# Spreading the inverse RMS roots of a decoder block: transpose, mask and one matmul of ones in place of eight matmuls

## The chip, the cores and the metric

The kernel runs on one core of a Trainium2 chip. The metric is the device time of one execution in microseconds (us). TensorE (PE) does matmuls and transposes, VectorE (DVE), ScalarE (ACT) and GpSimd (POOL) do elementwise work, and SyncE (SP) starts most DMAs. Each engine works through its own queue in order.

## The reference

One layer with 2048 tokens and 1024 channels, in float32. All four RMS norms have this form, over 1024 or 512 channels:

```python
def rmsnorm(x, g):
    r = lax.rsqrt(jnp.mean(xf * xf, axis=-1, keepdims=True) + EPS)
    return xf * r * g

hn = rmsnorm(h, norm1_g)
proj = einsum('bsd,de->bse', hn, w_in)          # u_pool | q | k | v, 512 channels each
y_pool = pool_mixer(u_pool, pool_w, pool_scale) # causal means over 2, 4, 8, 16 tokens, then 128x128 maps
y_attn = stick_breaking_attention(q, k, v)      # 8 heads of 64
mixed = concat[rmsnorm(y_pool, pool_out_g), rmsnorm(y_attn, attn_out_g)]
h = h + mixed @ w_out
up = rmsnorm(h, norm2_g) @ w_up                 # 4096 channels
h = h + square(relu(up)) @ w_down
return rmsnorm(h, final_g)
```

## The kernel before, in words

Channels lie on the 128 partitions and tokens on the free axis. The 2048 tokens are cut into `NT = 4` chunks of `T = 512`, and each chunk into `TB = 4` blocks of 128. A float32 product is made of three matmuls in the type fp32r: each operand is split by `split` (L145 on ACT, L146 on DVE) into a high and a low part, and high*high, high*low and low*high are summed (L177 to L179). In the text such a matmul of 512 columns, `pd<-h,hl`, is called a dense one.

The program has three stages. The front (to about 500 us) makes the input projection of all chunks, the pool mixer and the near part of the attention, interleaved. Then comes the output projection (to about 690 us), and then the two feed-forward products (names `pY`, `pZ`, `pX`, `pb`).

A norm goes like this. `sum_squares` adds squares over the channel tiles into `ss` (128 x 512). `mean_squares` (L204) makes four matmuls of one column each, which leave the mean square of each token in `pm`, 128 x 4: the tokens of a block are now on the partitions. `inv_root` copies it to SBUF on DVE (`v`, L212) and takes the inverse root in steps of Newton on POOL (L213 to L223). `inv_rms` splits the root into a high and a low part, `yr` (128 x 2 x 4, L240 and L241). `spread` (L230) turns this back into a row of 512 tokens that stands on every partition, `pr` in PSUM, by eight matmuls: for each block and part a column of `yr`, broadcast over 128 columns, is the stationary operand and the identity `identr` the moving one. ACT copies `pr` to `r` in SBUF (L250). `normed` then multiplies the chunk by gain and `r` on DVE (`nt`, L262) and splits it into `h` or `mix`.

In the executed path `inv_rms` runs 14 times: once on DVE alone (the first norm of chunk 0) and 13 times with POOL: norm 1 of chunks 1 to 3, the pool norm and the attention norm of four chunks each, and norm 2 of chunks 0 and 1. The other norms (norm 2 of chunks 2 and 3, the final norm) call `spread` themselves.

The order of instructions on each engine is worked out ahead of time by the framework's list scheduler, from its own estimates; it follows data dependencies, free buffers, priorities (`tc.high_priority` around `inv_rms`) and explicit orders (`tc.issue_after`). Two devices of the kernel set the order around the norms:

- `later` is a queue of small pieces of norm work, of which one to three are written after each projection step.
- `gates` holds pairs of a step count and an instruction: a projection step whose count is past the pair's may only be issued behind that instruction. `inv_rms` gates on its last `pm` matmul (10 granules on) and on its last spread matmul (14 on).

PSUM tiles come from pools with few buffers: `pd` 2, `pz` 2 (attention logits), `pt` 2 (attention transposes `pta`, and `pr`), `px` 1 (`pp` of the pool mixer, transposes of v, `pm`), `po` 1. For chunk 1 (`early`) `pr` comes from `pz` in place of `pt`.

Other names in the rows: `raw` and `hl` are weights before and after their split, `pls` and `pp` input and output of the pool mixer's matmul (L396 to L398), `yb` its copy by ACT (L399), `qkr` and `qk` queries and keys, `kw`, `qa`, `qb`, `sh`, `sg`, `pc`, `at`, `vw` operands and results of the attention, `acc` the residual.

Of the kernel before, what the change touches and what calls it, by code (L numbers as in the profile page):

```python
# [8 lines left out]
F32 = mybir.dt.float32  # L9
F32R = mybir.dt.float32r  # L10
BF16 = mybir.dt.bfloat16
I32 = mybir.dt.int32
AF = mybir.ActivationFunctionType
ALU = mybir.AluOpType

P = 128
S = 2048
D = 1024
T = 512
# [8 lines left out]
TB = T // P  # L28
# [17 lines left out]
def hymba_block(ctx: ExitStack, tc: tile.TileContext, xT, gains, w_in, pool_w, w_out, w_up, w_down, out):  # L46
    nc = tc.nc
# [3 lines left out]
    const = pool("const", 1)  # L51
    vp = pool("vp", 2)
    dram = pool("dram", 1, space=bass.MemoryType.DRAM)
    wp = hpb = hpa = pa = bigp = x0p = ntp = tmp = att = psd = psx = psz = pst = pso = olp = accp = acc2p = acc3p = None

    def open_pools(scope):
        nonlocal hpb, wp, tmp, ntp, psd, psx, psz, pst, pso
        fpool = lambda name, bufs, **kw: scope.enter_context(tc.tile_pool(name=name, bufs=bufs, **kw))
        hpb = fpool("hpb", KD, side="right")
        ntp = fpool("ntp", 3, side="right")  # L60
        tmp = fpool("tmp", 2, side="right")
        wp = fpool("wp", 2, side="right")
        psz = fpool("psz", 2, space=PS)
        pso = fpool("pso", 1, space=PS)
        psd = fpool("psd", 2, space=PS)
        psx = fpool("psx", 1, space=PS)
        pst = fpool("pst", 2, space=PS)
# [19 lines left out]

    front_scope, left_scope, att_scope, out_scope, last_scope, inner = (ctx.enter_context(ExitStack()) for _ in range(6))
    open_pools(front_scope)
    open_big(left_scope)  # L90

# [3 lines left out]
    ident = const.tile([P, P], F32, name="ident")  # L95
    make_identity(nc, ident)
    identr = const.tile([P, P], F32R, name="identr")
    nc.vector.tensor_copy(identr, ident)
    const.tile([P, P // 2], F32, name="gap")
    later_keys = const.tile([P, 2, 2, P], mybir.dt.int8, name="later_keys")  # L100
    nc.gpsimd.memset(later_keys, 0.0)
    for i in range(2):
# [49 lines left out]
    marks, gates = {}, []  # L152
# [46 lines left out]
    def mean_squares(parts, n, where=None, tag="px"):  # L199

        pm = (where or psx).tile([P, T], F32, tag=tag, name="pm")
        for c in range(TB):
            for i, ss in enumerate(parts):
                marks["pm"] = nc.tensor.matmul(pm[:, c:c + 1], ss[:, c * P:(c + 1) * P], inv[n],  # L204
                                               start=(i == 0), stop=(i == len(parts) - 1))
        return pm[:, 0:TB]

    def inv_root(pm, eng):

        v, w = vp.tile([P, 3 * TB], F32, tag="v", name="v"), pm.shape[-1]  # L210
        m, y, t = v[:, 0:w], v[:, TB:TB + w], v[:, 2 * TB:2 * TB + w]
        nc.vector.tensor_scalar(m, pm, 1.0, EPS, op0=ALU.mult, op1=ALU.add)  # L212
        eng.tensor_scalar(y.bitcast(I32), m.bitcast(I32), -0.5, float(0x5F3759DF), op0=ALU.mult, op1=ALU.add)  # L213
        for _ in range(3):
            if eng is nc.vector:
                eng.scalar_tensor_tensor(t, y, -0.5, y, op0=ALU.mult, op1=ALU.mult)
                eng.tensor_tensor(t, t, m, ALU.mult)
                eng.scalar_tensor_tensor(y, t, 1.5, y, op0=ALU.add, op1=ALU.mult)
            else:
                eng.tensor_tensor(t, y, y, ALU.mult)  # L220
                eng.tensor_tensor(t, t, m, ALU.mult)
                eng.tensor_scalar(t, t, -0.5, 1.5, op0=ALU.mult, op1=ALU.add)
                eng.tensor_tensor(y, y, t, ALU.mult)  # L223
        return y

    def spread(pr, yr):

        for b in range(TB):
            for x in range(2):
                mm = nc.tensor.matmul(pr[:, b * P:(b + 1) * P], yr[:, x, b:b + 1].to_broadcast([P, P]), identr,  # L230
                                      start=(b == 0 and x == 0), stop=(b == TB - 1 and x == 1), skip_group_check=True)
        return mm

    def inv_rms(ss, n, r=None, eng=None, early=False):

        eng = eng or nc.gpsimd
        with tc.high_priority():
            y = inv_root(mean_squares([ss], n, psz if early else None, "pz" if early else "px"), eng)
            yr = tmp.tile([P, 2, TB], F32R, tag="yr", name="yr")
            eng.tensor_copy(yr[:, 0], y)  # L240
            eng.tensor_tensor(yr[:, 1], y, yr[:, 0].bitcast(F32), ALU.subtract)  # L241
            where, tag = (psx, "px") if eng is nc.vector else (psz, "pz") if early else (pst, "pt")
            pr = where.tile([P, T], F32, tag=tag, name="pr")
            marks["pr"] = spread(pr, yr)
            if eng is not nc.vector:
                g = state["tick"]
                gates.extend([(g + 10, marks["pm"]), (g + 14, marks["pr"])])
            if r is None:
                r = tmp.tile([P, T], F32, tag="r", name="r", bufs=2)
            nc.scalar.activation(r, pr, AF.Copy)  # L250
            return r

    def rms(chunks):
        return inv_rms(sum_squares(chunks), len(chunks) * P)
# [41 lines left out]
    todo, begun, finished, state = [], {}, set(), {"gran": 0, "tick": 0, "due": 0.0}  # L296
# [37 lines left out]
    def norm1_first():  # L334

        x, h = st[0]["x"], []
        for k in range(KD):
            d = make_h(0)
            a = nc.scalar.activation(d[:, 0], x[:, k], AF.Copy, scale=g1[:, k:k + 1])
            v = nc.vector.scalar_tensor_tensor(d[:, 1], x[:, k], g1[:, k:k + 1], d[:, 0].bitcast(F32),  # L340
                                               op0=ALU.mult, op1=ALU.subtract)
            h.append((d[:, 0], d[:, 1]))
        st[0]["h"] = h
        with tc.issue_after(a.ins), tc.issue_after(v.ins):
            ss = sum_squares([x[:, k] for k in range(KD)])
        st[0]["r"] = inv_rms(ss, D, root_tile(), nc.vector)

    def norm1_rms(j):
        def square(k):
            if k == 0:  # L350
                st[j]["ss"] = sum_tile()
            add_square(st[j]["ss"], st[j]["x"][:, k], k == 0)
        later.extend(lambda k=k: square(k) for k in range(KD))
        later.append(lambda: st[j].update(r=inv_rms(st[j]["ss"], D, root_tile() if j == 2 else None, early=j == 1)))
# [1217 lines left out]
    pa = inner.enter_context(tc.tile_pool(name="pa", bufs=2))  # L1572
    x0p = x0_scope.enter_context(tc.tile_pool(name="x0p", bufs=2, side="right"))
# [69 lines left out]
```

## Time and profile before

| what | value |
|---|---|
| runs of the kernel before | 1900.64, 1901.84, 1903.91 us (median 1901.84) |
| profiled execution | 1901.53 us, of it 1899.8 us span from first to last instruction |
| PE busy | 1873.7 us, 99% |
| DVE, ACT, POOL busy | 1482.2 us (78%), 1025.0 us (54%), 235.1 us (12%) |
| mean granted TensorE clock | 0.996 |
| matmuls of `spread` | 152 (136 on `yr`, 16 on `yrlast`) |

A row of the groups reads: line, engine, operation, out<-in by the program's names, shapes, count | busy us, mean ns of one | idle us of the engine just before, and what ended it. A row of the timeline reads: start in us, length in us, engine, line, operation, count, and in brackets how long the engine had been idle and for whom. The length of a matmul runs to its modelled end, and the next one starts before that; what one costs in a row is the distance of starts.

### The profile page before, as it was taken

How to read it: one execution, taken by the hardware profiler on the slowest of the kernel's cores; microseconds unless marked ns; L12 is line 12 of the kernel's file. 1: busy time of each engine (PE TensorE's matmuls, PEld its weight loads, DVE VectorE, ACT ScalarE, POOL GpSimd, SP SyncE). 2: the span in 40 equal slices, each digit the busy share in tenths (PEclk: the TensorE clock that was granted, in tenths of full speed). 3: DMA queues.
4: the chain of work that ended last, by engine and by line, in shares of the span. 5: the costliest groups of instructions: out<-in, count | busy, mean ns of one | idle time of the engine just before them, and what ended most of it. 6: DMA issues, size and time to landing. Idle time of an engine off the chain costs nothing.

```text
span 1899.8 us, 26686 instructions
## 1 busy us (share of the span) xinstructions
PE 1873.7 (99%) x8883; PEld 1563.1 (82%) x8883; DVE 1482.2 (78%) x2151; ACT 1025.0 (54%) x1616; POOL 235.1 (12%) x463
## 2 busy tenths in 40 slices
PE   9999999999999999999999999999999999999997
PEld 7888888888888888788888888888888888888886
DVE  6887799668866976878799988887666677888774
ACT  6565566555544465455557555554432665656543
POOL 0333234223321020000000000000010010020120
PEclk9999999999999999999999999999999999999998
DMA  7685686898788867787899897889999899999852
GB/s 227 206 282 180 215 278 221 255 322 265 271 300 324 295 233 245 279 316 271 292 358 338 315 302 280 300 280 333 389 309 341 274 321 306 330 302 344 286 209 91
DMA packets 222164, 535.91 MB, mean 282 GB/s; under 512 B 26048, under 2 KB 32192, under 8 KB 218176
## 3 DMA queue, kind: packets, MB, share of 16 engines
q1 hardware_dynamic: 217264, 525.46, 79.4%
q0 software_dynamic: 4608, 8.39, 2.4%
q8 instruction: 72, 1.18, 0.3%
q14 instruction: 76, 0.62, 0.1%
q10 hardware_dynamic: 144, 0.26, 0.0%
HBM read 349.46 MB, written 184.55 MB: 281 GB/s over the span
## 4 chain that ended last, share of the span: by engine, by line
PE 52%; DMA 3%; DVE 2%; issue 1%; ACT 1%; POOL 0%; SPq 0%; DVEq 0%; ACTq 0%
PE pb L1274 16%; PE pY L1101 13%; PE pb L1451 12%; PE pZ L1101 7%; PE pX L1101 3%; DMA hn<-hs 1%; PE pb L1391 1%; DMA su<-hs 0%; DMA td<-t 0%; DMA wr<-in_w_down_dram 0%; DMA b<-in_w_down_dram 0%; DMA ar<-sd 0%; DMA t<-in_w_down_dram 0%; DVE hw L146 0%; DVE a L1060 0%
## 5 line engine op out<-in xcount | busy, mean ns | idle before, releaser
L1101 PE MATMUL pY<-sa,hw 128*128 128x512 f32 x1536 | 366.4, 389 | 2.6 <-ACT u L1024 2.6
L1101 PEld LDWEIGHTS pY<-sa,hw 128*128 128x128 f32 x1536 | 287.9, 188 | 64.0 <-ACT u L1024 4.3
L1274 PE MATMUL pb<-ad,wd 128*128 128x512 f32 x1344 | 304.8, 389 | 0.0
L177 PE MATMUL pd<-h,hl 128*128 128x512 f32 x752 | 298.4, 397 | 1.8 <-ACT vf L437 0.7
L179 PE MATMUL pd<-h,hl 128*128 128x512 f32 x752 | 296.5, 394 | 0.0
L178 PE MATMUL pd<-h,hl 128*128 128x512 f32 x752 | 296.3, 394 | 0.0
L1274 PEld LDWEIGHTS pb<-ad,wd 128*128 128x128 f32 x1344 | 252.3, 188 | 52.4
L1451 PE MATMUL pb<-ad,wd 128*128 128x512 f32 x1104 | 253.8, 390 | 0.6 <-ACT ad L145 0.6
L1451 PEld LDWEIGHTS pb<-ad,wd 128*128 128x128 f32 x1104 | 206.5, 188 | 44.3 <-ACT ad L145 1.0
L146 DVE TENSOR_TENSOR ad<-ar,ad 128x1024 fp32r<-128x1024 f32 x160 | 194.2, 1221 | 41.3 <-ACT ad L145 40.9
L145 ACT ACTIVATE ad<-ar 128x1024 fp32r<-128x1024 f32 x160 | 168.2, 1053 | 91.0 <-PE pb L1451 32.0
L1101 PE MATMUL pZ<-sa,hw 128*128 128x512 f32 x768 | 187.0, 390 | 1.8 <-DVE a L1044 1.8
L1101 PEld LDWEIGHTS pZ<-sa,hw 128*128 128x128 f32 x768 | 143.8, 188 | 33.1 <-DVE a L1044 3.4
L177 PEld LDWEIGHTS pd<-h,hl 128*128 128x128 f32 x752 | 142.1, 189 | 29.8 <-ACT h L145 1.1
L179 PEld LDWEIGHTS pd<-h,hl 128*128 128x128 f32 x752 | 141.8, 189 | 28.5
L178 PEld LDWEIGHTS pd<-h,hl 128*128 128x128 f32 x752 | 142.0, 189 | 26.5
L145 ACT ACTIVATE hl<-raw 128x512 fp32r<-128x512 f32 x168 | 104.0, 630 | 105.6 <-PE pd L179 66.7
L146 DVE TENSOR_TENSOR hl<-raw,hl 128x512 fp32r<-128x512 f32 x168 | 114.3, 686 | 46.1 <-ACT hl L145 41.4
L1018 ACT ACTIVATE a<-a 128x512 f32<-128x512 f32 x96 | 60.1, 629 | 93.1 <-DVE a L1060 40.0
L146 DVE TENSOR_TENSOR hw<-rt,hw 128x512 fp32r<-128x512 f32 x128 | 86.6, 686 | 24.7 <-ACT hw L145 24.6
L145 ACT ACTIVATE wd<-wq 128x1024 fp32r<-128x1024 f32 x56 | 59.4, 1060 | 79.6 <-PE pb L1274 69.2
L146 DVE TENSOR_TENSOR wd<-wq,wd 128x1024 fp32r<-128x1024 f32 x56 | 68.5, 1224 | 35.7 <-ACT wd L145 35.6
(218 smaller groups left out, 2749.3 us busy)
## 6 DMA issues: line engine op xcount, KB each, us to landing
ar<-sd SPq DMA_DIRECT2D x96, 512.0 KB, 5.6
ar<-sdi SPq DMA_DIRECT2D x64, 512.0 KB, 5.6
rb<-in_w_up_dram SPq DMA_DIRECT2D x30, 1024.0 KB, 6.3
sd<-a SPq DMA_DIRECT2D x104, 256.0 KB, 5.1
raw<-in_w_in_dram SPq DMA_DIRECT2D x50, 512.0 KB, 4.4
sdi<-hr SPq DMA_DIRECT2D x96, 256.0 KB, 5.5
wr<-in_w_down_dram SPq DMA_DIRECT2D x48, 512.0 KB, 5.4
sd<-s SPq DMA_DIRECT2D x88, 256.0 KB, 5.0
```

The costliest lines, as they stand in the source:

```text
L145: nc.scalar.activation(hi, src, AF.Copy)
L146: return nc.vector.tensor_tensor(lo, src, hi.bitcast(F32), ALU.subtract)
L177: nc.tensor.matmul(ps, hl[:, 0, c], hi, start=(k == 0), stop=False)
L178: nc.tensor.matmul(ps, hl[:, 0, c], lo, start=False, stop=False)
L179: mm = nc.tensor.matmul(ps, hl[:, 1, c], hi, start=False, stop=(k == n - 1))
L1018: nc.scalar.activation(t, src, AF.Relu)
L1101: nc.tensor.matmul(t, w[:, wx, c], a[:, ax, c % 2], start=first and c == 0 and x == 0, stop=last and c == G - 1 and x == 2, skip_group_che ...
L1274: nc.tensor.matmul(b, t[:, wx, 2 * (kk % 2) + c, i * P:(i + 1) * P], a[:, ax, c], start=p in ("P1", "P5", "P2") and kk == 0 and c == 0 and ...
L1391: nc.tensor.matmul(b[:, cols], block(t, wx, c, n), a[:, ax, c, cols], start=False, stop=(i == 1 and c == 1 and x == 2), skip_group_check=True)
L1451: nc.tensor.matmul(ps[q, n], block(t, wx, c, n), left_[q][:, ax, c], start=(n_ in ("P1", "P3") and kk == 0 and c == 0 and x == 0), stop=(n ...
```

## The change

The 13 calls of `inv_rms` with POOL no longer call `spread` but a new function, `spread_rows`. It transposes `yr`, read as 128 x 8, to 8 rows of 128 tokens (`pr[0:8, 0:128]`, mark `pt8`). ACT copies these rows four times into `roots`, 8 x 512, once for each block of tokens, each time scaled per row by a column of `sel`, which is one for the two rows (high and low) of that block and zero for the others. One matmul with ones, 8 rows and 512 columns, sums the eight rows onto all partitions, into the same tile `pr`. The copy from `pr` to `r` stays. The gate on the last spread matmul moves from 14 to 16, and the transpose gets a gate at 14. The DVE variant, `root_last` and the final norm keep `spread`. Two small constants, `sel` and `oner`, are made by DVE at the start; `gap` shrinks by as much, so that other constants keep their places. `roots` has a pool of its own of 2 KB per partition.

```diff
+        zp = fpool("zp", 1, side="right")
...
-    const.tile([P, P // 2], F32, name="gap")
+    const.tile([P, P // 2 - 8], F32, name="gap")
+    sel = const.tile([P, TB], F32, name="sel")
+    nc.vector.tensor_tensor(sel, ident[:, 0:TB], ident[:, TB:2 * TB], ALU.add)
+    oner = const.tile([P, TB], F32R, name="oner")
+    nc.vector.tensor_scalar(oner, sel, 0.0, 1.0, op0=ALU.mult, op1=ALU.add)
...
+    def spread_rows(pr, yr, r, mark):
+
+        rows, z = 2 * TB, zp.tile([P, T], F32R, tag="roots", name="roots")[0:2 * TB]
+        mm = nc.tensor.transpose(pr[0:rows, 0:P], yr.bitcast(F32).rearrange("p x b -> p (x b)"), ident)
+        marks[mark] = mm
+        for b in range(TB):
+            nc.scalar.activation(z[:, b * P:(b + 1) * P], pr[0:rows, 0:P], AF.Copy, scale=sel[0:rows, b:b + 1])
+        mm = nc.tensor.matmul(pr, oner[0:rows, 0:1].to_broadcast([rows, P]), z, start=True, stop=True)
+        nc.scalar.activation(r, pr, AF.Copy)
+        return mm
...
             pr = where.tile([P, T], F32, tag=tag, name="pr")
-            marks["pr"] = spread(pr, yr)
-            if eng is not nc.vector:
-                g = state["tick"]
-                gates.extend([(g + 10, marks["pm"]), (g + 14, marks["pr"])])
             if r is None:
                 r = tmp.tile([P, T], F32, tag="r", name="r", bufs=2)
-            nc.scalar.activation(r, pr, AF.Copy)
+            if eng is nc.vector:
+                marks["pr"] = spread(pr, yr)
+                nc.scalar.activation(r, pr, AF.Copy)
+            else:
+                marks["pr"] = spread_rows(pr, yr, r, "pt8")
+                g = state["tick"]
+                gates.extend([(g + 10, marks["pm"]), (g + 14, marks["pt8"]), (g + 16, marks["pr"])])
             return r
```

The scheduler works out a new order from this. In the rows below, lines of the changed program are 5 higher than before in the products (L182 to L184 for L177 to L179) and 18 higher from the pool mixer on (L414 to L416 for L396 to L398); L242 is the transpose, L245 the masking, L246 the matmul of ones, L247 the copy to `r`.

On PE, around the first of the 13 (norm 1 of chunk 1), there stands before, with the spread (L230) in the middle:

```order
L178 MATMUL pd<-h,hl 128x512
L179 MATMUL pd<-h,hl 128x512
L230 MATMUL pr<-identr,yr 128x128
L177 MATMUL pd<-h,hl 128x512
L230 MATMUL pr<-identr,yr 128x128 x7
L396 MATMUL pp<-pls,pw 128x512
L397 MATMUL pp<-pls,pw 128x512
L398 MATMUL pp<-pls,pw 128x512
L178 MATMUL pd<-h,hl 128x512
L179 MATMUL pd<-h,hl 128x512
```

At the same place now, with 16 dense matmuls and one `pp` group between the transpose (not shown) and the matmul of ones:

```order
L184 MATMUL pd<-h,hl 128x512
L246 MATMUL pr<-roots,oner 128x512
L414 MATMUL pp<-pls,pw 128x512
L415 MATMUL pp<-pls,pw 128x512
L416 MATMUL pp<-pls,pw 128x512
L414 MATMUL pp<-pls,pw 128x512
L415 MATMUL pp<-pls,pw 128x512
L416 MATMUL pp<-pls,pw 128x512
L182 MATMUL pd<-h,hl 128x512 x2
L183 MATMUL pd<-h,hl 128x512
```

Two groups of `pp`, which share one buffer, now follow each other, and the first of the two L182 is the first matmul that reads the `h` made with this `r`; before, one `pp` group, 17 dense matmuls and another `pp` group stood between the spread and it.

On ACT, at the same place, before:

```order
L145 ACTIVATE pls<-pl 128x512
L145 ACTIVATE hl<-raw 128x512
L250 ACTIVATE r<-pr 128x512
L399 ACTIVATE yb<-pp,gains 128x512
L145 ACTIVATE h<-nt 128x512 x3
L399 ACTIVATE yb<-pp,gains 128x512
```

And now:

```order
L150 ACTIVATE hl<-raw 128x512
L245 ACTIVATE roots<-pr,sel 8x128 x4
L417 ACTIVATE yb<-pp,gains 128x512
L150 ACTIVATE pls<-pl 128x512
L247 ACTIVATE r<-pr 128x512
L150 ACTIVATE qk<-qkr 128x512
L417 ACTIVATE yb<-pp,gains 128x512
L150 ACTIVATE h<-nt 128x512 x2
L417 ACTIVATE yb<-pp,gains 128x512
```

The four masks stand where the copy to `r` stood; that copy now stands behind a `yb` and a `pls`, and a `qk` and a `yb` stand between it and the first `h`.

On POOL, at the end of the root chain of the eighth of the 13 (the attention norm of chunk 1), before:

```order
L223 TENSOR_TENSOR v<-v 128x4
L647 AFFINE_SELECT sg<-sg 128x2x128
L220 TENSOR_TENSOR v<-v 128x4
L659 COPY left_140<-pc 128x2
L221 TENSOR_TENSOR v<-v 128x4
L222 TENSOR_SCALAR v<-v 128x4
L223 TENSOR_TENSOR v<-v 128x4
L240 CAST yr<-v 128x4
L241 TENSOR_TENSOR yr<-v,yr 128x4
```

And now:

```order
L228 TENSOR_TENSOR v<-v 128x4
L225 TENSOR_TENSOR v<-v 128x4
L226 TENSOR_TENSOR v<-v 128x4
L227 TENSOR_SCALAR v<-v 128x4
L228 TENSOR_TENSOR v<-v 128x4
L256 CAST yr<-v 128x4
L257 TENSOR_TENSOR yr<-v,yr 128x4
```

A mask and a copy of the attention, L647 and L659, which stood inside this chain now stand elsewhere. The feed-forward stage has the same order on PE as before, apart from where the two `spread` of `yrlast` stand at its start.

4 lines of the change are left out of this document (2 added, 2 removed).

## The prediction

> **What bounds the kernel now.** I read the page's first part, then the waits of PE, then PE's timeline around the spreads.
>
> ```profile
> span 1899.8 us, 26686 instructions
> PE 1873.7 (99%) x8883; PEld 1563.1 (82%) x8883; DVE 1482.2 (78%) x2151; ACT 1025.0 (54%) x1616; POOL 235.1 (12%) x463
> ...
> PE pY L1101 <- ACT u L1024: 2.6, 4, 1.0
> PE pr L230 <- POOL yr L240: 1.8, 1, 1.8
> PE pZ L1101 <- DVE a L1044: 1.8, 3, 1.0
> ```
>
> PE is busy for 99% of the span and its longest waits (us in total, times, longest) are a few us over the whole program. So what PE no longer issues is saved in full, as long as no new wait takes its place; work of the other engines is free while PE has something to do. One of these few waits is a spread that waits 1.8 us for POOL, and it has a sequel:
>
> ```profile
> 442.67 0.95 PE L204 MATMUL pm<-inv,ss 128*128 128x1 f32 x8
> ...
> 450.93 0.45 PE L179 MATMUL pd<-h,hl 128*128 128x512 f32 x1
> 453.20 2.03 PE L230 MATMUL pr<-identr,yr 128*128 128x128 f32 x8 [1.82 <-POOL yr L240]
> 455.03 1.07 PE L663 MATMUL pta<-ident,sg 128*128 128x128 f32 x4
> 455.76 0.78 PE L177 MATMUL pd<-h,hl 128*128 128x512 f32 x1
> 456.33 0.63 PE L178 MATMUL pd<-h,hl 128*128 128x512 f32 x1
> 456.76 0.63 PE L179 MATMUL pd<-h,hl 128*128 128x512 f32 x1
> ...
> 450.00:452.00 2.00, 1.38 (x12) 1.07 (x10) 1.52 (x3) 1.22 (x2) 1.83 (x7) 1.00 0.97 300
> 452.00:454.00 2.00, 0.80 (x4) 0.77 (x4) 1.09 (x2) 0.00 (x0) 1.77 (x5) 0.82 0.93 342
> 454.00:456.00 2.00, 2.00 (x11) 2.00 (x11) 1.90 (x4) 0.60 (x1) 0.00 (x0) 0.50 0.77 249
> 456.00:460.00 4.00, 4.00 (x11) 3.13 (x11) 3.26 (x5) 1.24 (x2) 0.00 (x0) 0.50 0.83 253
> 460.00:464.00 4.00, 4.00 (x23) 3.38 (x23) 1.35 (x2) 2.50 (x5) 0.34 (x1) 0.99 0.48 134
> ```
>
> The third number from the end of a row of stretches is the granted clock. It is 1.00 up to 452, then falls to 0.50 and is back shortly after 460: 0.72 us of the second stretch, all 6 of the next two and 0.08 of the last, 6.8 us at half speed with PE full of work (11 matmuls in 4 us against 23). That costs 3.4 us. It begins right behind the wait of 1.82 us, and it is the only such stretch that I found in the front and the output projection.
>
> **What is removed: the eight matmuls.** There are 13 places.
>
> ```profile
> 619.61 0.39 PE L179 MATMUL pd<-h,hl 128*128 128x512 f32 x1
> 619.83 1.00 PE L230 MATMUL pr<-identr,yr 128*128 128x128 f32 x8
> 620.67 0.45 PE L177 MATMUL pd<-h,hl 128*128 128x512 f32 x1
> 620.96 0.39 PE L178 MATMUL pd<-h,hl 128*128 128x512 f32 x1
> 621.19 0.39 PE L179 MATMUL pd<-h,hl 128*128 128x512 f32 x1
> ```
>
> Starts of dense matmuls are 0.23 us apart (620.96 to 621.19). From 619.83 to 620.96 PE passes eight spread matmuls and one dense: 1.13 less 0.23 is 0.90 us a place.
>
> **What is added on PE: a transpose and a matmul of 512 columns.** The nearest rows are the transposes of the attention, which run in groups of four:
>
> ```profile
> 184.85 0.63 PE L663 MATMUL pta<-ident,sg 128*128 128x128 f32 x4
> 185.23 0.48 PE L396 MATMUL pp<-pls,pw 128*128 128x512 f32 x1
> 185.54 0.39 PE L178 MATMUL pd<-h,hl 128*128 128x512 f32 x1
> ```
>
> Four take 0.38 us, 0.10 each, and the matmul behind them takes 0.31 in place of 0.23, so a change of kind costs some 0.08. One transpose by itself is at least 0.10 and at most the whole 0.46 of such a group. I take 0.18, one transpose and one change, since the moving operand has the same 128 columns. The matmul of ones streams 512 columns like a dense one; only its depth of 8 rows has no row here. It is 0.23 at least and 0.31 at most (the one behind a change of kind); I take 0.25, as its neighbours are of its kind. Together 0.43 (0.33 to 0.77). **Each place saves 0.47 us (0.13 to 0.57), all 13 save 6.1 us (1.7 to 7.4).**
>
> **The four masks on ACT**, and what waits for them.
>
> ```profile
> L663 PE MATMUL pta<-ident,sg 128*128 128x128 f32 x248 | 40.8, 278 | 0.6 <-DVE sg L658 0.6
> L187 ACT ACTIVATE sq<-yb 128x512 f32<-128x512 f32 x18 | 11.1, 628 | 0.7 <-DMA yb<-os 0.7
> L399 ACT ACTIVATE yb<-pp,gains 128x512 f32<-128x512 f32 x16 | 11.0, 689 | 9.3 <-PE pp L398 9.0
> L250 ACT ACTIVATE r<-pr 128x512 f32<-128x512 f32 x12 | 7.2, 599 | 21.7 <-PE pr L230 21.6
> L1398 ACT ACTIVATE sqh<-u 128x256 f32<-128x256 f32 x8 | 3.3, 418 | 7.2 <-DVE u L1396 4.4 <-DVE v L216 2.0 <-DVE v L218 0.8
> ```
>
> No activation of 8x128 exists before. 512 columns take 628 ns and 256 take 418, so 128 would take some 313; a scale by a column adds 90 (689 against 599, both from PSUM). About 0.4 us each, 1.6 for four; at most four times 0.69, 2.8. With the transpose (0.28) the rows are ready 1.9 us after it starts (at most 3.1). In the new order 10 dense matmuls stand between transpose and matmul of ones at the closest place (the sixth), 2.3 us, and 16 to 28 matmuls and more at the others, so PE doesn't wait for the masks, and at the upper price 0.8 us at one place. ACT's 21 us more (13 times 1.6) lie in an engine that is busy 54% and that already idled 21.6 us ahead of `r` for the spread. Behind the masks in its queue stand mostly splits of weights (`hl`), which are made five granules ahead, 60 dense matmuls or 13.7 us; that is the cover, and I cost them at nothing. DVE gets two 128x4 operations at the start, ahead of the first input. No DMA is added; the `mix` DMAs start as much later as `r` does, and are read a stage later.
>
> **A later `r`.** It now comes 2.3 to 6.8 us of PE work behind the transpose. In the order PE first reads the `h` of the other norms 21 us or more after the matmul of ones, or through DRAM, so the delay is covered there. It is not at the first of the 13. In the trace of before PE worked 5.3 us of other matmuls between that spread and the first `h`:
>
> ```profile
> 68.65 0.89 PE L230 MATMUL pr<-identr,yr 128*128 128x128 f32 x7
> 69.38 0.45 PE L396 MATMUL pp<-pls,pw 128*128 128x512 f32 x1
> ...
> 74.67 0.40 PE L177 MATMUL pd<-h,hl 128*128 128x512 f32 x1
> ...
> 77.94 0.50 PE L177 MATMUL pd<-h,hl 128*128 128x512 f32 x1 [0.70 <-DVE qkr L423]
> ...
> 69.58 0.60 ACT L250 ACTIVATE r<-pr 128x512 f32<-128x512 f32 x1 [1.79 <-PE pr L230]
> ```
>
> Now two `pp` groups stand there and nothing else, 1.4 us, and the second needs the buffer of the first, which `yb` on ACT frees. ACT does `r`, `qk`, `yb` in this order. Counted from the start of the matmul of ones: 0.39 to its end (as a dense one), 0.60 for `r`, some 0.6 for `qk` (as `r`), 0.69 for `yb`, 2.3 us; PE has issued its own four matmuls by 0.9. It waits 1.4 us. (At least 0.8, if `yb` goes as soon as `pp` ends; 2.0 if the first `h` must be through too.) The dense matmul that waited 0.70 us for `qkr` at 77.94 is likely covered, as DVE's new order has that `qkr` ahead of `nt`. **+1.4 and -0.7.**
>
> **Where the roots are waited for.** The transposes need `yr` as the spread did.
>
> ```profile
> 453.23 0.20 POOL L241 TENSOR_TENSOR yr<-v,yr 128x4 fp32r<-128x4 f32 x1
> ...
> 610.49 0.20 POOL L241 TENSOR_TENSOR yr<-v,yr 128x4 fp32r<-128x4 f32 x1
> ...
> 612.13 0.56 PE L230 MATMUL pr<-identr,yr 128*128 128x128 f32 x4
> ...
> 444.03 0.63 ACT L145 ACTIVATE hl<-raw 128x512 fp32r<-128x512 f32 x1 [4.01 <-DMA raw<-in_w_in_dram]
> ```
>
> At the eighth place (442.67 to 453.20) the new order has 34 dense matmuls between `pm` and the transpose where 19 stood, and fewer of the attention (four transposes at 0.10, four of 128 columns at 0.06, five of 256 at 0.12, by their share of a dense one): 15 times 0.23 less 1.2, so PE arrives 2.2 us later, beyond the 1.82 it waited. POOL's chain also loses the two attention steps inside it. So this wait goes, **-1.8 us**, and with it the half-speed stretch behind it, **-3.4 us**. The late `raw` of 444.03, which held ACT and with it the root's first step, may come again; the later arrival still covers it. At the twelfth (`yr` ready at 610.69, spread at 612.13, 1.44 to spare) eight dense matmuls fewer, 1.8 us, stand ahead: **+0.4 us**.
>
> **Sum**: -6.1 - 1.8 - 3.4 + 1.4 - 0.7 + 0.4 = -10.2 us. The profiled execution took 1901.53 (span 1899.8 and 1.7 around it), 0.3 below the median 1901.84. 1901.5 - 10.2 = 1891.3 us.
>
> **A rule against the trace.** The Trainium skill, "TensorE: Matmul & The Clock Gate", section "Why this matters for your kernels", says that only gaps of more than about 3 us between bursts drop the clock. Here half speed stands right behind a wait of 1.82 us, so by the trace a shorter one was enough, at least beside sparse matmuls; waits of 1.0 us had no such sequel. By the page the stretch at 453 would have another cause and stay, and the sum would be 3.4 us higher, 1894.7; that is the first rival.
>
> **Rivals.**
> - The half-speed stretch stays at 453, or comes behind another wait, the 1.4 us of the first place above all. For it: waits of 1.0 us and 1.82 us bracket 1.4, so it can't be excluded. Against: around it PE has only dense work. 1894.7, and 1896.5 if the old wait stays too.
> - The change saves nothing that can be measured: transpose and matmul of ones cost 0.77 a place and the old wait stays. 1901.5 - 1.7 + 1.1 = 1900.9. For it: eight matmuls already overlap weight load and stream; against: 0.46 for one small transpose is a whole group's price.
> - Slower: PE, which issues in order, now stands at two points a place for another engine, POOL and then ACT, where it stood at one. Where a mask sits in ACT's queue behind a split that waits for its `raw` (4.01 us at 444.03), PE stands at the matmul of ones and half speed follows: some 1.5 + 3.4 = 4.9 us each. If that happens at three places (the sixth, and the ninth and twelfth, whose masks follow three splits in a row) while the old wait stays, 1901.5 - 6.1 + 1.1 + 14.7 = 1911.2; one place about undoes the gain (1901.4), and from the second on (1906.3) the kernel is slower. Against: elsewhere some 4 to 6 us stand between transpose and matmul of ones.
>
> **How the numbers follow.** Forecast 0.50, first rival 0.25, no change 0.14, slower 0.11. A measurement here tells about 0.2%, 3.8 us, from no change: faster is below 1898.0, slower above 1905.6. Forecast and first rival are faster: 0.75. The low end, with the cheapest transpose (-7.4) and the smallest new wait (0.8, and none at the twelfth), is 1901.5 - 7.4 - 5.2 - 0.7 + 0.8 = 1889.0; the high end takes in the first rival and half of the second. 1888.5 to 1900.
>
> **What the profile after would show.** PE's starts around a transpose some 0.18 apart beyond the dense pitch, and the matmul of ones at 0.25; 78 fewer matmuls; masks of about 0.4 us; no wait for `yr` and clock 1.00 at the eighth place; a wait of `pp` for `yb` of about 1.4 us near 70 us; feed-forward stages of the same length. The forecast is wrong if half speed shows anywhere before 690 us, if `pr<-roots` has waits for ACT, or if a transpose takes over 0.4.

## The result and the profile after

The change makes the kernel slower: 1927.64 us median (1923.20 to 1930.29, 5 runs) against 1902.85 (median of 5 runs of the kernel before, the three shown above among them), a ratio of 1.0135 (95% interval 1.0121 to 1.0148). The profiled execution took 1925.68 us. Its page, with the engines' busy time:

```profile
span 1924.0 us, 26571 instructions
PE 1881.5 (98%) x8805; PEld 1559.6 (81%) x8805; DVE 1482.9 (77%) x2153; ACT 1038.0 (54%) x1668; POOL 223.0 (12%) x463
```

PE has 78 matmuls fewer and is busy 7.8 us longer; the span is 24.2 us longer. So PE stands idle for more of the time, and part of its work runs at a lower clock. Two stretches of the front show where, first of the kernel before and then of the kernel after (the columns: length, PE, PEld, DVE, ACT, POOL busy with counts, granted clock, DMA share, GB/s):

```profile
80.00:480.00 400.00, 394.66 (x2169) 339.29 (x2168) 325.37 (x492) 236.89 (x439) 126.33 (x229) 0.99 0.78 252
480.00:720.00 240.00, 239.58 (x1166) 201.30 (x1165) 186.62 (x280) 122.99 (x203) 50.01 (x125) 1.00 0.77 276
```

```profile
80.00:480.00 400.00, 377.77 (x1999) 319.00 (x1998) 305.71 (x462) 227.87 (x435) 106.06 (x213) 0.97 0.72 235
480.00:720.00 240.00, 238.58 (x1145) 196.31 (x1144) 186.35 (x281) 124.12 (x226) 48.37 (x124) 1.00 0.80 285
```

Between 80 and 480 us PE idles 22.2 us where it idled 5.3, and the clock is 0.97 for 0.99. With the first 80 us and the last 240, idle time to 720 us is 26.6 in place of 9.1, 17.6 more. The lower clock adds 8.5: before 720 us the trace shows five stretches at half speed, 23.9 us in all, where the kernel before had one of 6.8, and a microsecond at half speed loses half of itself. Against that stand some 2 us that the new instructions save (below): 24, close to the whole loss. The feed-forward products begin 26.2 us later (715.8 for 689.6) and take 2 us less than before. The longest waits of PE in the kernel after (us in total, times, longest):

```profile
PE pp L415 <- DVE pls L151: 5.2, 2, 3.5
PE po L692 <- DVE ot L652: 4.1, 1, 4.1
PE po L692 <- ACT at L150: 2.7, 1, 2.7
PE po L692 <- DVE at L151: 2.6, 2, 2.4
PE pp L414 <- ACT pls L150: 2.6, 3, 1.6
PE pd L182 <- DVE qk L151: 1.7, 2, 1.5
...
PE pr L242 <- POOL yr L257: 1.0, 1, 1.0
```

None of the large ones is at the new instructions. PE waits for operands of the pool mixer (`pls`) and of the attention (`at`, `ot`, `qk`), mostly from DVE. The wait of 1.0 us for `yr` is the only one at a transpose.

The last of the 13 places shows what the new instructions cost and where they stand, on PE and then on ACT:

```profile
645.69 0.39 PE L182 MATMUL pd<-h,hl 128*128 128x512 f32 x1
645.91 0.27 PE L242 MATMUL pr<-ident,yr 128*8 128x128 f32 x1
645.94 0.48 PE L183 MATMUL pd<-h,hl 128*128 128x512 f32 x1
646.26 0.40 PE L184 MATMUL pd<-h,hl 128*128 128x512 f32 x1
646.49 0.39 PE L182 MATMUL pd<-h,hl 128*128 128x512 f32 x1
...
651.48 0.39 PE L183 MATMUL pd<-h,hl 128*128 128x512 f32 x1
651.80 0.49 PE L246 MATMUL pr<-roots,oner 8*128 8x512 f32 x1
652.22 0.50 PE L184 MATMUL pd<-h,hl 128*128 128x512 f32 x1
652.55 0.39 PE L182 MATMUL pd<-h,hl 128*128 128x512 f32 x1
652.78 0.40 PE L183 MATMUL pd<-h,hl 128*128 128x512 f32 x1
```

```profile
646.28 1.11 ACT L245 ACTIVATE roots<-pr,sel 8x128 fp32r<-8x128 f32 x4 [0.39 <-PE pr L242]
...
652.41 0.58 ACT L247 ACTIVATE r<-pr 128x512 f32<-128x512 f32 x1
```

The transpose takes 0.12 us of PE's row (646.49 less 645.69 is 0.80; three dense matmuls take 0.68), the matmul of ones 0.62 (1.30 for three dense ones and itself). The masked rows are ready at 647.39. The matmul of ones starts at 651.80, 25 dense matmuls and 5.9 us behind the transpose and 4.4 us after its operand was there; no wait precedes it, PE does the 25 dense matmuls that stand ahead of it in the row. So `r` comes later in PE's row. By the count of dense matmuls that PE had started when ACT's `r` began, `r` is 17 to 36 dense matmuls later than before at the eleven of the 13 places whose row is called `r<-pr` (at the two others it is `ra<-pr`, and the delay is 28 and 21), 26 in the mean, 6.0 us at 0.2275 us each.

What a late `r` does shows at the fourth place. The kernel before, where `r` starts at 235.55, in the 12 us ahead of it and the 16 behind:

```profile
224.00:236.00 12.00, 12.00 (x70) 10.49 (x69) 4.95 (x8) 4.96 (x9) 3.57 (x17) 1.00 0.88 296
236.00:252.00 16.00, 15.29 (x86) 12.99 (x85) 15.83 (x23) 12.62 (x25) 6.12 (x6) 1.00 1.03 349
```

and the kernel after, where it starts at 250.17, with two of PE's rows there:

```profile
236.00:250.00 14.00, 14.00 (x72) 11.59 (x71) 6.45 (x10) 7.66 (x17) 3.19 (x11) 1.00 1.01 361
250.00:268.00 18.00, 12.29 (x64) 10.42 (x63) 17.22 (x26) 12.64 (x24) 2.50 (x6) 0.87 0.77 265
```

```profile
263.21 1.54 PE L692 MATMUL po<-at,vw 128*128 128x256 f32 x6 [4.09 <-DVE ot L652]
...
266.22 0.80 PE L182 MATMUL pd<-h,hl 128*128 128x512 f32 x1 [1.46 <-DVE qk L151]
```

DVE's queue in the kernel after between the coming of `r` and the end of PE's wait, in part (DVE has no pause between these rows):

```profile
252.01 2.22 DVE L280 SCALAR_TENSOR_TENSOR nt<-yb,gains,r 128x512 f32<-128x512 f32 x3
254.16 1.21 DVE L667 TENSOR_TENSOR_SCAN pc<-sh,later_keys 128x512 f32<-128x512 f32 x1
...
257.67 0.68 DVE L676 TENSOR_TENSOR sg<-sg,pc 128x510 f32<-128x510 f32 x1
...
258.87 0.74 DVE L280 SCALAR_TENSOR_TENSOR nt<-yb,gains,r 128x512 f32<-128x512 f32 x1
...
262.51 0.65 DVE L652 TENSOR_TENSOR ot<-ot,po 64x512 f32<-64x512 f32 x1
```

In both kernels DVE has little to do until `r` comes (41% and 46% busy) and then works almost without a pause, at the normed tiles and at the attention's `pc`, `sg`, `at`, `ot`, `qk` that come in the same queue. In the kernel before PE has other work for nearly all of that burst. In the kernel after PE is 25 dense matmuls further on when the burst begins, and comes to matmuls that read `at`, `ot` and `qk` before DVE has made them: 4.09 and 1.46 us.

Not every wait goes this way. Behind the third place's `nt` and `h` PE waits 1.71 us for `pls` (ends at 214.00), and behind the seventh's `nt` and `mix` 2.71 us for `at` (ends at 422.05); with the two above that is 10.0 us. But the 2.39 us that end at 105.64 lead to POOL: `at` needs `sg`, whose mask POOL starts at 104.21, right behind the root chain of the second place (its last step, L257, starts at 104.06). And no `nt` stands in DVE's queue from 340 to the end of two waits for `pls`, 1.62 and 3.52 us (at 352.86 and 356.89). Whether those two go back to a late `r` was not followed.

### The profile page after: what moved, and what is told of

It reads as the page before. It is cut to its first block, busy times and chain, and to the rows that moved or that the text cites. A ratio compares the mean times of both kernels' runs of the same rounds, so it can differ in the third digit from the quotient of the medians.

```text
span 1924.0 us, 26571 instructions
## 1 busy us (share of the span) xinstructions
PE 1881.5 (98%) x8805; PEld 1559.6 (81%) x8805; DVE 1482.9 (77%) x2153; ACT 1038.0 (54%) x1668; POOL 223.0 (12%) x463
## 4 chain that ended last, share of the span: by engine, by line
PE 87%; DVE 5%; DMA 3%; POOL 1%; ACT 1%; issue 1%; SPq 0%; DVEq 0%; ACTq 0%; POOLq 0%
PE pY L1119 18%; PE pb L1292 16%; PE pb L1469 11%; PE pZ L1119 9%; PE pd L182 7%; PE pd L183 7%; PE pd L184 7%; PE pX L1119 4%; PE po L692 1%; PE pta L681 1%; DVE hl L151 1%; PE pm L209 1%; PE pb L1409 1%; PE pz L634 1%; DMA sr<-su 1%
## 5 line engine op out<-in xcount | busy, mean ns | idle before, releaser
L182 PE MATMUL pd<-h,hl 128*128 128x512 f32 x752 | 299.1, 398 | 3.4 <-DVE qk L151 1.7
L184 PE MATMUL pd<-h,hl 128*128 128x512 f32 x752 | 298.9, 397 | 0.9 <-DVE hl L151 0.9
L182 PEld LDWEIGHTS pd<-h,hl 128*128 128x128 f32 x752 | 143.5, 191 | 33.5 <-DVE qk L151 2.6
L184 PEld LDWEIGHTS pd<-h,hl 128*128 128x128 f32 x752 | 143.1, 190 | 30.9 <-DVE hl L151 1.4
```

The lines of the kernel that those rows point to most:

```text
L182: nc.tensor.matmul(ps, hl[:, 0, c], hi, start=(k == 0), stop=False)
L184: mm = nc.tensor.matmul(ps, hl[:, 1, c], hi, start=False, stop=(k == n - 1))
```

## The experiments

Each run stands against runs of the kernel before on the same chip. "r late" is the mean of the count just described, in us at 0.2275 a dense matmul; the last column is the stretch from 80 to 480 us.

| run | median us | ratio to before (95%) | r late, us | PE busy of 400 us, matmuls, clock |
|---|---|---|---|---|
| before (first group) | 1902.88 | 1 | 0 | 394.7, 2169, 0.99 |
| after | 1927.64 | 1.0135 (1.0121 to 1.0148) | 6.0 | 377.8, 1999, 0.97 |
| e5 transpose, eight matmuls at once | 1899.87 | 0.9983 (0.9973 to 0.9994) | 0.5 | 395.1, 2190, 1.00 |
| e6 masks, eight matmuls behind | 1935.93 | 1.0175 (1.0158 to 1.0192) | 5.3 | 382.6, 2050, 0.97 |
| e7 masks aside | 1903.68 | 1.0004 (0.9991 to 1.0017) | -0.1 | 393.2, 2155, 0.99 |
| e8 longer chain on POOL | 1933.51 | 1.0165 (1.0130 to 1.0200) | 3.7 | 382.6, 2063, 0.98 |
| e9 held buffer | 1917.07 | 1.0084 (1.0062 to 1.0107) | uneven | 388.7, 2137, 0.99 |
| e11 r by DMA | 1928.40 | 1.0147 (1.0130 to 1.0164) | 3.8 (see there) | 383.4, 2085, 0.98 |
| e12 before, other order | 1902.89 | 0.9999 (0.9983 to 1.0015) | 0.0 | 395.8, 2190, 1.00 |
| e13 after, other order | 1929.70 | 1.0145 (1.0124 to 1.0166) | 4.9 | 381.4, 2027, 0.97 |
| e3 rows in px | 1951.33 | 1.0261 (1.0238 to 1.0284) | 6.0 | 382.9, 2024, 0.97 |
| e10 one copy | 1937.85 | 1.0190 (1.0164 to 1.0216) | 5.0 | 376.5, 1998, 0.97 |
| e14 after, early roots | 1909.02 | 1.0024 (1.0009 to 1.0039) | 3.9 | 390.6, 2110, 0.99 |
| e15 before, early roots | 1901.09 | 0.9983 (0.9972 to 0.9993) | -3.5 | 397.1, 2196, 1.00 |
| e16 after, low halves on POOL | 1932.67 | 1.0141 (1.0114 to 1.0169) | 5.7 | 380.0, 2004, 0.97 |
| e17 before, low halves on POOL | 1911.89 | 1.0039 (1.0024 to 1.0053) | -1.1 | 391.0, 2138, 0.99 |
| e19 after, low halves left out | 1922.81 | 1.0097 (1.0071 to 1.0123) | 5.5 | 385.9, 2082, 0.99 |
| e20 before, low halves left out | 1900.05 | 0.9993 (0.9981 to 1.0006) | -1.1 | 395.0, 2183, 1.00 |

The letters of the theories: L, the late `r`; I, the new instructions; A, ACT's load; H, the held PSUM buffer; P, PE's waits for GpSimd; O, an unlucky order; M, the masks' length; S, the length of the chain of roots at any time; D and G, how lateness costs; E, any relief of DVE.

### Which part of the change

e5, on the kernel after:

```
         mm = nc.tensor.transpose(pr[0:rows, 0:P], ...)
-        for b in range(TB):
-            nc.scalar.activation(z[:, b * P:(b + 1) * P], ..., scale=sel[0:rows, b:b + 1])
-        mm = nc.tensor.matmul(pr, oner[0:rows, 0:1].to_broadcast([rows, P]), z, start=True, stop=True)
+        mm = spread(pr, yr)
```

> The kernel after with the transpose of the roots, and the old eight matmuls right behind it in place of masks and matmul of ones (the transposed rows are overwritten and not used). Theory L (lateness): the time is lost because the matmul of ones stands some 25 dense matmuls behind the transpose and r comes 5 to 6 us later at nearly every place; here r is not late, so PE only pays 13 more transposes of 0.12 us (its place among the dense ones in the trace of after), 1.6 us: about 1903, and between 1896 and 1906 since the order moves a little. Rival I (the new instructions themselves): a transpose with the 8 columns and its change of stationary operand costs far more than its slot shows; then most of the 24 us stays: 1915 to 1928.

1899.87 us: the transposes are innocent, and 3 us are even gained; the eighth place's wait and its half-speed stretch are gone here (clock 1.00). e6 keeps the masks and changes only the last line:

```
-        mm = nc.tensor.matmul(pr, oner[0:rows, 0:1].to_broadcast([rows, P]), z, start=True, stop=True)
+        mm = spread(pr, yr)
```

> The kernel after with transposes and masks, and the eight old matmuls behind the masks in place of the one matmul of ones (the masked rows are not read). Theory L: r is as late as in after, and PE pays eight matmuls (0.90 us) for one (0.52) at 13 places, 5 us: 1920 to 1934. Rival I (the matmul of ones, 8 rows deep, is what costs): the loss goes with it: 1908 or less.

1935.93, just above the range of L: the matmul of ones isn't the cause either. Between e5 and e6 only the step through ACT differs, and with it the place of the eight matmuls and the time for which `pr` is held: 36 us. e7 gives ACT nearly the same work outside the chain (0.25 us an activation, without a scale by a column, for 0.35), in the kernel before:

```
             nc.scalar.activation(r, pr, AF.Copy)
+            if eng is not nc.vector:
+                z = tmp.tile([P, T], F32R, tag="roots", name="roots")[0:2 * TB]
+                for b in range(TB):
+                    nc.scalar.activation(z[:, b * P:(b + 1) * P], pr[0:2 * TB, 0:P], AF.Copy)
```

> The kernel before, with four activations of 8x128 added behind r at each of the 13 places, whose output nobody reads: ACT's new load without the chain (13 times 1.1 us, the four masks' length in after). Theory L: nothing waits for them, 1897 to 1905. Rival A (ACT's load delays the splits of weights and the rest of ACT's queue): a loss of 10 us or more, 1911 to 1926.

1903.68, no change: ACT's load costs nothing that can be measured. So it is not any one instruction but the step between two of PE's, and where the second stands.

### Lateness or the held buffer

e8, on the kernel before:

```
+            for _ in range(0 if eng is nc.vector else 12):
+                eng.tensor_scalar(y, y, 1.0, 0.0, op0=ALU.mult, op1=ALU.add)
             eng.tensor_copy(yr[:, 0], y)
```

> The kernel before, with 12 steps more on GpSimd (y times 1 plus 0) in the chain of roots at each place: r comes later by 12 times 0.28 us (the steps' distance from 175.92 to 177.03 in the trace of before) to 12 times 0.36 us (their mean at busy places), 3.4 to 4.3 us, with no mask, no transpose, no longer hold of a PSUM buffer and no work for PE. Theory L: 3.4 to 4.3 of 5.5 us late costs 62 to 78% of the 24 us, 15 to 19 us: 1914 to 1922. Rival H (the PSUM buffer of pr, held 7 us in place of 2, is what costs) and rivals I and A: about as before, 1898 to 1906.

1933.51, more than L said. The run isn't clean, as its waits of PE show:

```profile
PE pr L230 <- POOL yr L242: 7.0, 7, 2.2
PE pta L665 <- DVE sg L656: 2.9, 1, 2.9
```

7.0 us are PE's own waits for the longer chain at the spread, which the kernel after hardly has; the 2.9 us for `sg` go back to POOL as well, where the mask for `sg` (starts at 107.00) stands among the added steps. e11 leaves the instructions of PE and POOL and the PSUM tiles as they were:

```
-            nc.scalar.activation(r, pr, AF.Copy)
             ... (with POOL only)
+            r0 = tmp.tile([P, T], F32, tag="r0", name="r0", bufs=2)
+            nc.scalar.activation(r0, pr, AF.Copy)
+            nc.scalar.dma_start(r, r0)
```

> The kernel before, where ACT writes the spread roots to another tile and a DMA, issued from ACT right behind, copies this to r: r is later by one DMA of 256 KB (3.6 us for vs<-vt to 5.1 us for sd<-a, median from issue to landing in the trace of before), while PE, GpSimd, DVE and the PSUM buffers have exactly the old work and PE waits for no root longer than before. Theory L: 3.6 to 5.1 of 5.5 us late costs two thirds to nearly all of the 24 us: 1916 to 1927. Rivals H, I and A, and a rival P for the last run of late roots (that PE's waits for GpSimd cost there, not the late r): 1898 to 1907.

The DMA's row (KB, median us to landing) and DVE's wait for it:

```profile
r<-r ACTq DMA_DIRECT2D x11, 256.0 KB, 3.4
```

```profile
DVE nt L267 <- DMA r<-r: 10.7, 7, 4.9
```

With 3.4 us from issue to landing, and the issue 1.0 us after the start of a copy that itself takes 0.6, `r` is some 3.8 us late, and the kernel takes 1928.40: as much as the whole loss of the change, without a transpose, a mask, a longer hold of `pr` or a long wait of PE for a root. P, H, I and A don't explain it, and its 13 DMAs move 3.4 MB beside the 536 MB of the whole kernel. (The order moved a little: PE stands up to 9 dense matmuls away from before when ACT copies `pr`.) PE's waits also stand at nearly the same spots: 1.96 us to 106.69, 1.91 to 213.95, 2.10 and 3.06 to 266.05, where the kernel after has 2.39 to 105.64, 1.71 to 214.00, 4.09 and 1.46 to 266.22. So a late `r` alone brings these about, the one that leads to POOL too. None stands near 355; one of 2.39 (to 375.28) does instead. e9 asks for the hold alone:

```
             ... (and `mean_squares` writes into the tile that it is given)
+            pr = where.tile([P, T], F32, tag=tag, name="pr")
-            y = inv_root(mean_squares([ss], n, psz if early else None, "pz" if early else "px"), eng)
+            y = inv_root(mean_squares([ss], n, pr), eng)
```

> The kernel before, where the mean squares (pm) go to the first columns of the PSUM tile that the spread later fills (pr), so that one of the attention's buffers is held from the mean squares to r, some 10 us instead of 2, while the spread itself, its eight matmuls and r stay where they were in PE's row. Theory L (only the lateness of r costs): as before, 1896 to 1906. Rival H (the held buffer costs, 7 us instead of 2 at 13 places of after for 24 us): with 10 us at least as much, 1918 to 1932.

1917.07, between the two. It doesn't decide: the new place of `pm` moved the order, so that `r` is 29 dense matmuls later than before at one place and 52 earlier at another. e3 takes the hold of the attention's buffer away, holds that of `px` in its place, and keeps the lateness:

```
+        pq = psx.tile([P, T], F32, tag="px", name="pq")
-        mm = nc.tensor.transpose(pr[0:rows, 0:P], ...)
+        mm = nc.tensor.transpose(pq[0:rows, 0:P], ...)
             ... (masks read pq)
+        pr = new_pr()
```

> The kernel after with the transposed rows in the PSUM tile of the mean squares (px), so that the attention's buffer (pr) is held only from the matmul of ones to r, some 1 us, shorter than before; the distance from transpose to matmul of ones, and so the lateness of r, stays. Theory L (lateness by itself): at least 1918, and up to 1940 since px is one buffer and the next mean squares then wait for it. Rival H (the 14 us that a held buffer cost in the run with pm and pr in one tile are also most of the loss of after): 1912 or less.

1951.33: worse than L's range. The hold of the attention's buffer is not needed for a loss; the one buffer of `px` is a worse place still, so that the run can't tell what lateness alone does. How much the hold adds in the kernel after stays open.

### Chance of the order

e12 and e13 change one line of the kernel before and of the kernel after:

```
-RATIO_FRONT = (0.3, 0.4, 0.15, 0.4, 0.4, 0.3)
+RATIO_FRONT = (0.28, 0.34, 0.15, 0.34, 0.42, 0.34)
```

> The kernel before with other numbers for how much attention work goes between the granules of dense work (RATIO_FRONT 0.28, 0.34, 0.15, 0.34, 0.42, 0.34 for 0.3, 0.4, 0.15, 0.4, 0.4, 0.3): a neutral reshuffle, roots on time. Theory L: within 10 us of before, 1892 to 1910. Rival O (the old order was tuned for the old instructions, and any reshuffle costs this much): 1912 or more.

> The kernel after with the same other numbers as the last run. Theory L: r is as late as in after, so the loss against the old kernel with these numbers stays 15 to 30 us: 1910 to 1932. Rival O (after only met an unlucky order): 1906 or less, and nearer than 10 us to the old kernel with these numbers.

1902.89 and 1929.70: with the other numbers the two kernels stand 27 us apart, as with the old ones. The loss isn't an accident of the one order; other orders were not tried.

### The chain's length

e10, on the kernel after:

```
-        for b in range(TB):
-            nc.scalar.activation(z[:, b * P:(b + 1) * P], pr[0:rows, 0:P], AF.Copy, scale=sel[0:rows, b:b + 1])
-        mm = nc.tensor.matmul(pr, oner[0:rows, 0:1].to_broadcast([rows, P]), z, start=True, stop=True)
         ... (`selr` is `sel` in fp32r)
+        nc.scalar.activation(z[:, 0:P], pr[0:rows, 0:P], AF.Copy)
+        for b in range(TB):
+            mm = nc.tensor.matmul(pr[:, b * P:(b + 1) * P], selr[0:rows, b:b + 1].to_broadcast([rows, P]), z[:, 0:P], ...)
```

> The kernel after with one copy of the transposed rows (8x128) in place of four masks, and four matmuls of 128 columns, each with a column of the masks as its stationary operand, in place of the matmul of ones. ACT's part of the chain is a quarter of the old 1.1 us. Theory L as I hold it (what costs is that the last matmul stands 20 to 25 dense ones behind the transpose, whatever ACT really needs between): 1915 to 1930. Rival M (the four masks' length and their place in ACT's queue make r late): 1912 or less.

1937.85, above both ranges. On ACT and on PE, at the twelfth place:

```profile
641.61 0.27 ACT L246 ACTIVATE roots<-pr 8x128 fp32r<-8x128 f32 x1 [3.49 <-PE pr L244]
```

```profile
641.30 0.27 PE L244 MATMUL pr<-ident,yr 128*8 128x128 f32 x1
...
646.28 0.66 PE L248 MATMUL pr<-roots,selr 8*128 8x128 f32 x4
```

ACT is done at 641.88, 0.6 us after the transpose, and PE's four matmuls still stand 5.0 us behind it. M falls: what ACT needs doesn't set the distance, the order does. (Why the scheduler keeps it, and why this run is 10 us slower than the kernel after, was not found.) e14 and e15 shorten the other end of the chain; they leave out the Newton steps, so their roots are rough:

```
-        for _ in range(3):
+        for _ in range(3 if eng is nc.vector else 0):
```

> The kernel after without the Newton steps of GpSimd's roots (only the first guess is left, so the roots are rough): 12 steps of 0.28 to 0.36 us less in the chain, 3.4 to 4.3 us, with the transpose, masks, matmul of ones and held buffer all there. r is then only 1 to 2 us later than in before. Theory L: most of the loss goes, 1896 to 1908. Rival H (the buffer is held just as long) and rival I: 1915 to 1928.

> The kernel before without the Newton steps of GpSimd's roots, the control of the run above: r is 3.4 to 4.3 us earlier than in before. Theory L says that a root on time gains little by being earlier, save at the few norms of the end where PE waits for the root itself: 1890 to 1903. A rival S (every microsecond of the chain of roots is worth some 4 to 7 us of the span, early or late): 1875 to 1888.

The kernel after with early roots takes 1909.02, 1 us above L's range: 20 of the 25 us are back, with transpose, masks, matmul of ones and the held buffer all in place. So these together cost little by themselves, against I and H. But `r` is still 3.9 us late here, where 1 to 2 were expected, so that L doesn't give the number. The kernel before gains 3 us, so S falls; a root that is on time gains little by being earlier. The edit does a second thing: it takes twelve steps a place out of POOL's queue, in which the attention's masks stand too. The wait of 2.39 us that led to POOL is gone in e14. How much of the 20 us comes this way can't be told, as the kernel before has no such wait that e15 could lose.

### How lateness becomes waits

If PE waits for DVE's burst, less work for DVE must help the kernel after and not the kernel before. e16 and e17 move the subtractions:

```
-            split((d[:, 0], d[:, 1]), t)
+            nc.scalar.activation(d[:, 0], t, AF.Copy)
+            nc.gpsimd.tensor_tensor(d[:, 1], t, d[:, 0].bitcast(F32), ALU.subtract)
```

> The kernel after with the low halves of the normed tiles (h and mix, 56 subtractions of 128x512, 0.60 us apart on DVE) made by GpSimd in place of DVE: 34 us less on DVE, most of it in the stretches behind each r. Theory D (the part of L on how lateness costs: behind the late r the normed tiles and the attention's steps meet on DVE, which then runs without a pause while PE waits for it): a part of the 24 us comes back, 1904 to 1918. Rival G (PE waits for the late r's own chain or for held buffers, DVE's load is not the limit): no gain, 1922 to 1930, or more, since the trace has no 128x512 on GpSimd (its 128x256 takes 0.99 us) and h and mix come later.

> The kernel before with the same low halves on GpSimd: the control. Its PE waits 7.5 us in all before 720, of it some 3 for DVE, so theory D gives at most these and the half-speed stretch: 1890 to 1902, and a smaller gain than the kernel after has from it. Rival G: no gain, 1900 to 1908, or slower where GpSimd is slow.

1932.67 and 1911.89, neither gains, as G has it. The group of e16 says why the pair is not clean:

```profile
L283 POOL TENSOR_TENSOR h<-nt,h 128x512 fp32r<-128x512 f32 x32 | 55.7, 1760 | 31.9 <-ACT h L282 31.8
```

POOL takes 1.76 us for what takes DVE 0.68, so `h` itself comes later. e19 and e20 use ACT and leave the low halves out:

```
+            nc.scalar.activation(d[:, 1], t, AF.Copy, scale=0.0)
```

> The kernel after with zeros written by ACT in place of the low halves of h and mix (the low halves are left out of the result): DVE is relieved as in the first of these runs, with an operation whose length is known (0.63 us, a copy of 128x512 on ACT), and 35 us more on ACT, which is busy 54%. Theory D: 1904 to 1918. Rival G: 1922 to 1932.

> The kernel before with zeros written by ACT in place of the low halves of h and mix (left out of the result): the control of the same edit to the kernel after, where PE's waits before 720 us fell from 25.1 to 16.8 us. Theory D (DVE's load behind a late r is what PE waited for): in the kernel before, whose waits there are 7.5 us, the edit gives at most 5 us: 1896 to 1906. Rival E (less work on DVE makes either kernel faster by as much, and says nothing of the late r): 15 us or more in the front, 1880 to 1892.

e19 takes 1922.81, short of D's range and in G's; e20 1900.05, no change. So by the time D failed. Its trace, read after the result, shows the front and the end apart:

```profile
80.00:480.00 400.00, 385.89 (x2082) 327.93 (x2081) 295.87 (x440) 256.07 (x495) 102.78 (x224) 0.99 0.76 245
```

```profile
PE pr L235 <- POOL yrlast L839: 6.6, 1, 6.6
```

In the front PE gets through 83 matmuls more than the kernel after in the same time, at a clock of 0.99. Its 2200th dense matmul (of 2304) starts 8.8 us later than in the kernel before, against 25.6 in the kernel after: 17 us are back. Then one new wait of 6.6 us near 714, for the root of a last norm, and half speed behind it (10.2 us from 716.69) eat most of it. (The 16.8 us in the expectation of e20 leave this wait out, as it ends after 720.) In e20 the same count is 3.5 us earlier than before. So relief of DVE gives back the larger part of the loss in the front, and less where there was no loss (17 against 3.5 us): that speaks for D and against E, in one profiled execution of each kernel.

What stays open: lateness and loss don't lie on one curve (e14 and e11 are late by about the same and lose 5 and 25 us). That a late `r` is enough for the loss is shown, by e11; what share of it goes through DVE's queue, through POOL's or through the held buffer is not.

## Why the prediction was wrong

The forecast was 1891.3 us, in a range of 1888.5 to 1900; 1927.6 came.

- **A later `r`: the step that failed.** It asked when PE first reads the `h` that `r` makes, found 21 us and more, and costed 12 of the 13 places at nothing. But `r` is read by DVE first, and behind those `nt` in DVE's queue stand the attention's steps that PE needs much sooner. PE's idle time before the feed-forward stages grew by 17.6 us, most of it in waits for `pls`, `at`, `ot` and `qk`, and half speed behind them added 8.5; 10.0 us of the waits stand behind the `nt` of three places. The whole loss came back when a DMA made `r` alone late (e11). The forecast had this lateness in numbers ("2.3 to 6.8 us of PE work") and looked at the wrong reader.
- **The first place**: `pp` does wait for `yb` there, 0.89 us where 1.4 was forecast, and no half speed follows. Right in kind, and too small to matter. The 0.70 us for `qkr` near 78 us are gone, as forecast, and no wait came at the twelfth place, where 0.4 was forecast:

```profile
76.37 0.50 PE L414 MATMUL pp<-pls,pw 128*128 128x512 f32 x1 [0.89 <-ACT yb L417]
```

- **The transpose**: 0.12 us in the row for a forecast of 0.18. **The matmul of ones**: 0.62 for 0.25. The forecast took it for one more of its neighbours' kind; the distances of starts around it are 0.32, 0.42 and 0.33 in place of 0.23. (Whether its 8 rows are the reason was not tested.) A place costs 0.74 in place of 0.90, and all 13 save 2.1 us, not 6.1. 0.74 lies inside the forecast's 0.33 to 0.77. This term was mis-sized by 4 us, and for that alone the forecast would have been 1895.
- **The masks**: 0.35 us each and 1.1 for four, for 0.4 and 1.6. ACT has 13.0 us more, not 21, and it is hidden, as forecast (e7). PE never waits for a mask, so the rival that put the loss there is wrong in its mechanism; its sign was right.
- **The eighth place**: its wait for `yr` and the half speed behind it are gone, as forecast (the transpose starts at 484.86 without a wait). The seventh now has one of 1.0.
- **The rival of half speed behind another wait** was right in kind, but there are five such stretches, not one; they cost 8.5 us more than the one before. The page "TensorE: Matmul & The Clock Gate" of the Trainium skill names gaps of more than about 3 us (its section "Why this matters for your kernels"). In the kernel after, a wait of 2.39 us (ends at 105.64) is followed by half speed, one of 1.21 (ends at 143.69) is not; the stretches of each and behind it:

```profile
100.00:106.00 6.00, 3.61 (x28) 3.21 (x26) 3.00 (x7) 3.60 (x8) 4.60 (x16) 1.00 0.95 297
106.00:115.00 9.00, 9.00 (x47) 8.04 (x46) 7.20 (x11) 2.58 (x5) 1.14 (x3) 0.81 0.52 144
142.00:144.00 2.00, 0.79 (x6) 0.57 (x5) 1.76 (x4) 1.95 (x5) 0.45 (x2) 1.00 1.00 379
144.00:155.00 11.00, 11.00 (x60) 9.40 (x59) 10.94 (x18) 7.82 (x15) 1.46 (x3) 1.00 0.93 281
```

The second row's 0.81 over 9 us is 3.4 us at half speed. By that page of the Trainium skill only the waits of 4.09 and 3.52 us here would have a sequel; the trace shows one behind 1.71, 2.39 and 2.71 us too. What decides stands in the last section.

## What to carry to other kernels

When a change moves a result later, list every reader of it and what stands behind each reader in its engine's queue, and ask who waits for that; the first reader on the bounding engine is not enough. Removing instructions from the busiest engine can lose more than it saves if it puts one more trip to another engine into a chain, above all where the order is fixed ahead of time and the second half does not start when its operand is there (here 4.4 us later). To tell a late operand from dear instructions, delay the operand alone, by a DMA for example.

## What the runs showed of the hardware

- A matmul whose operands have 8 rows costs more in a dense row than one of 128 rows with the same 512 columns: 0.62 us against 0.23, of which 0.42 lie up to the next start and the rest at its two neighbours.
- Idle time of PE counts within steps of 3.413 us. In every trace here half speed begins at times that lie whole multiples of 3.413 us apart (in the kernel after 106.21, 215.44, 263.23, 355.39 and 423.65), and before the feed-forward stages it lasts one, two or three such steps. So the length of a wait alone does not decide: behind 1.82 us (before) and 2.39 (after) half speed came, while behind 1.96 us in e11 (104.73 to 106.69) and 3.02 in e19 (465.87 to 468.89) the clock stayed 1.00. The edge of a step cuts the 3.02 us into 1.64 and 1.38. Over the 18 traces, each step at full clock in which PE idled for 1.9 us or more was followed by half speed, none with less than 0.9 was, and between these it went either way.
- A 128x512 subtraction takes 1.67 to 1.76 us in the mean on GpSimd (e16, `mix` and `h`) and 0.68 on DVE.
